# A Strassen matmul with its own scheduler: DMA rates and queue shares by stage, s2 in a11's place, one more second-level product

## The chip, the cores and the metric

The kernel runs on one core of a Trainium2 chip. The metric is the device time in microseconds of one execution. A matmul's rate is set by TensorE (PE); VectorE (DVE) and ScalarE (ACT) make the operands and take the results out of the accumulator banks (PSUM); GpSimd (POOL) issues the loads of the fp32 inputs, which are cast to fp16 on their way into the on-chip memory; SyncE (SP) issues all other DMAs. Both issue to the same 16 DMA engines.

## The reference

```python
def reference(a, b, bias):          # a 4096 x 4096, b 4096 x 4096, float32
    return np.tanh(np.matmul(a, b) + bias)
```

## The kernel before

**The sums.** The output is made in four panels of 1024 columns. A panel's product is made by Winograd's form of Strassen's scheme: a pair of row tiles (2 x 128 rows) and the two halves of the inner dimension give a11, a12, a21 and a22, the panel gives b11 to b22, and with s1 = a21 + a22, s2 = s1 - a11, s3 = a11 - a21, s4 = a12 - s2 and t1 to t4 likewise there are seven products: P1 = a11 b11, P2 = a12 b21, P3 = s4 b22, P4 = a22 t4, P5 = s1 t1, P6 = s2 t2, P7 = s3 t3. Two pairs form a *duo*, which is worked on together. A product of a duo is 2 x 16 matmuls of 512 columns (`product`, L817). It can be split once more by the same scheme over the duo's two pairs (a *fine* or second-level product): seven parts p1 to p7 of eight matmuls of 256 columns each (`fine`, L848, and `fine_product`, L832). For that VectorE makes half sums of the left side (ya, za of a11; ys, zs of s3 and s1; `fine_left`, L663) and quarter sums of the right side (f1, f2, f4 and one in place; `fine_right`, L802).

**The stages.** The opening computes the first 1024 rows of the first panel in plain matmuls (L2041). Then six duos finish the first panel; `STEEP` (L63) says how many products of each duo are fine: none for the first, then P1, then P1 and P7, then P1, P7 and P5. The second and third panels are made together in *wide* passes (`wide_pass`, L1710; class `Wide`, L1542), all products fine, with 512 columns to a part; seven products of eight duos, 56 in all. The last panel runs in two passes (`pass_one`, L1353, and `pass_two`, L1436) with 256 columns to a part; in the tables below its start is at about 1083 us.

**A duo of the first panel** (`run_duo`, L1036). POOL loads rows of a ("nat"), VectorE turns them (STREAM_TRANSPOSE, L498) into a11, a12, a21, a22. The order of TensorE is P1 (with, when it is fine, a product of the duo before as a filler between its parts p2 and p4), a second product that was held back from the duo before, P2, P7 and P6 by turns, P5, and then the tail P3, P4, P4, P3, of which the last two are held back for the next duo. A fine P7 runs p1, p5, p7, p6, p2, then P6 of the first pair as its filler, then p4 and p3, then P6 of the second pair. Three small sums of 256 columns (`ps<-ps,parts`, `parts<-ps,parts`) after the parts p6 and p2 make the banks ready for p4. After P5, `after_p5` (L1017) adds p7 to the bank and so frees it for P3.

**What is stored.** For the later panels, a11, a12, a22 and s2 of each pair (and some half sums) are stored to device memory by SP (`keep`, L590; in the traces `a<-a`, `s<-s`, `a<-ya`). Before, s2 has a buffer of its own in `natural` (L547), and s4 is later made in s2's place (`work`, L938). VectorE must wait for the store before it writes there.

**What sets the order.** Every operation is recorded first, with the buffers that it reads and writes and an estimated duration. A planner (`Plan.schedule`, L237) then plays the program through: TensorE's order is fixed as recorded; every other engine takes the ready operation with the nearest due time that finds room in 51 places on chip (`fits`, L277). A DMA is modelled by a rate, a fixed wait, and, when POOL and SP both have transfers under way, by a share for each (`rates`, L297). The order that comes out is the program's order on each engine, and each engine then runs in that order. So numbers of the model do not change what is computed; they change what stands behind what. `NEAR` (L32) says how far ahead of the matmul a load of b stops competing for places with what is due sooner.

```python
            soft_, hard = pipes["POOL"], pipes["SP"]
            part = SHARE[hard[0][1].kind]
            return [(soft_, part), (hard, 1 - part)]
```

Of the kernel before, what the change touches and what calls it, by code (L numbers as in the profile page):

```python
# [10 lines left out]
P = 128  # L11
# [4 lines left out]
T = 16  # L16
TB = 4
# [32 lines left out]
PLAIN = (0, 0, 0, 0)  # L50
SMALL = 7
LONG = 1.07
OVER = False
TWICE = True
RING = 8
DMA = {'POOL': (382140.0, 3.8), 'LATER': (386100.0, 4.8), 'in': (372240.0, 4.6), 'out': (376200.0, 4.3), 'open': (368280.0, 4.2)}
# [17 lines left out]
WIDE_EARLY = {'P1': (11.0, 70), 'P2': (11.0, 80), 'P6': (11.0, 100), 'P7': (8.0, 120), 'P4': (11.0, 70), 'P5': (11.0, 50), 'P3': (18.0, 100)}  # L74

# [68 lines left out]
class Op:  # L144
    __slots__ = (
        "parts", "n", "eng", "dur", "lag", "emit", "preds", "succs", "bufs", "nbytes", "hw", "soft", "early", "lead", "reach", "far",
        "unsent", "flying", "flow", "wait", "kind",
        "due", "left", "start", "done", "ready",
# [3 lines left out]
class Plan:  # L152
# [13 lines left out]

    def add(self, eng, dur, emit, reads=(), writes=(), nbytes=0, hw=True, soft=None, early=0.0, lead=0.0, reach=1e9, after=None, faster=1.0):
        early, far = early if isinstance(early, tuple) else (early, self.FAR)
        op = Op()
# [67 lines left out]
    def schedule(self):  # L237
# [163 lines left out]
def kernel(  # L401
# [113 lines left out]

    def load_rows(tl, srcs, nbytes, lead=0.0, faster=1.0):
# [7 lines left out]
        add("POOL", 4 * 0.55, emit, (), (tl,), nbytes=nbytes, hw=False, lead=lead, faster=faster)  # L524

    def natural_rows(pair, r, s, soft=None):
# [4 lines left out]
        for u in range(2):  # L531
# [5 lines left out]

            load_rows(tl, srcs, P * T * P * 4, NAT_LEAD if soft else 0.0, LONG)
            for h, name in enumerate(names if r == 0 else names[::-1]):
# [6 lines left out]

    def natural(pair, kept, own=False, spare=()):  # L547
        s = {}
# [188 lines left out]

    def load_b(buf, c, k0, nt, j=None, early=0.0, faster=1.0):

# [4 lines left out]
        def emit():  # L744
# [9 lines left out]
            "POOL", 4 * 0.55, emit, (), (buf,),  # L754
            nbytes=nt * P * n * 4, hw=False, early=early, faster=faster,
        )
# [953 lines left out]
    def wide_pass(c, held):  # L1710
# [5 lines left out]
        def load(name, at_=parts):  # L1716
            r, j = int(name[1]) - 1, int(name[2]) - 1
            for blk, i in at_:
                if not i:
                    bufs = [new(name, [P, 2, 2, NB], atoms=2 * TB) for _ in range(2)]  # L1720
                    for h in range(2):
                        raw[name, blk, h] = Block(bufs, h)
                load_b(raw[name, blk, 0].bufs[i], c + j, r * T + blk * TB + 2 * i, 2, early=soon[0], faster=LONG)

# [254 lines left out]
    def both_columns(h, blk):  # L1979
# [4 lines left out]
        for i, buf in enumerate(bufs):  # L1984
            load_b(buf, 0, h * T + blk * TB + 2 * i, 2)

# [167 lines left out]
    for c in range(NC):  # L2154
# [44 lines left out]
        for i, pairs in enumerate(duos):  # L2199
# [75 lines left out]
```

## Time and profile before

| | before |
|---|---|
| median of 3 runs | 1440.67 us (1439.12 to 1443.03) |
| the profiled execution | 1442.41 us; its span 1440.7 us |
| TensorE busy | 1423.2 us, 8384 matmuls |
| VectorE, ScalarE, GpSimd busy | 1070.7, 389.2, 325.4 us |
| granted TensorE clock | 0.999 |
| HBM read, written | 329.25 MB, 150.21 MB |

The span runs from the first to the last instruction of one profiled execution. "x" counts instructions. A row of the timeline has the start, the time that the group took, the engine, the line, what is written and read, the count, and in brackets how long the engine had been idle before it and what ended that. Names like `parts` or `b_209` are those of the first buffer that held a place: another buffer can be in it by then.

### The profile page before, as it was taken

The numbers are of one execution on the slowest core, as the hardware profiler recorded it, in microseconds if no ns is written. First come the engines' busy times: TensorE is split into PE (matmuls) and PEld (weight loads), VectorE is DVE, ScalarE is ACT, GpSimd is POOL, SyncE is SP. The second block draws the span as 40 slices with busy tenths as digits, with TensorE's granted clock in tenths as the row PEclk, the third lists the DMA queues.
The fourth block names the chain that finished last, engine by engine and source line by source line (L and its number), as shares of the span: only waits on it lengthen the run. The fifth ranks groups of instructions, "written<-read, shape, count | busy, mean of one in ns | idle before, by whom it ended". The sixth has DMA issues, their size and how long they took to land.

```text
span 1440.7 us, 22498 instructions
## 1 busy us (share of the span) xinstructions
PE 1423.2 (99%) x8384; PEld 819.5 (57%) x8384; DVE 1070.7 (74%) x1587; ACT 389.2 (27%) x740; POOL 325.4 (23%) x613
## 2 busy tenths in 40 slices
PE   9999999999999999999999999999999999999998
PEld 4444545555544444444444444444446888888887
DVE  3349976767885576796567778988687689997866
ACT  3111211221233223311111133233323332234443
POOL 8754343144353341100112130000120220000000
PEclk9999999999999999999999999999999999999999
DMA  9999999698999999897889899899999898789873
GB/s 175 183 228 284 245 268 287 163 237 208 266 264 309 260 284 313 291 368 268 266 286 310 280 293 380 332 390 330 329 325 342 237 276 284 256 277 321 308 285 134
DMA packets 168062, 401.30 MB, mean 279 GB/s; under 512 B 25488, under 2 KB 44432, under 8 KB 167952
## 3 DMA queue, kind: packets, MB, share of 16 engines
q1 hardware_dynamic: 104976, 320.12, 61.0%
q0 software_dynamic: 62976, 79.73, 33.3%
q8 instruction: 66, 1.08, 0.3%
q14 instruction: 44, 0.36, 0.1%
HBM read 329.25 MB, written 150.21 MB: 333 GB/s over the span
## 4 chain that ended last, share of the span: by engine, by line
PE 76%; DMA 11%; DVE 3%; issue 1%; SPq 0%; POOL 0%; ACT 0%; DVEq 0%; POOLq 0%; ACTq 0%
PE ps L1564 44%; PE ps L839 25%; PE ps L824 6%; DMA b<-in_b_dram 3%; DMA a<-parts 2%; DMA s<-s 2%; DMA out_dram<-parts 1%; DMA nat<-in_a_dram 1%; DMA a<-o 1%; DVE a L498 1%; DMA s<-parts 1%; DVE parts L465 1%; DVE s L465 0%; SPq L586 0%; DVE ps L465 0%
## 5 line engine op out<-in xcount | busy, mean ns | idle before, releaser
L751 POOL DMA_DIRECT2D b<-in_b_dram x320 | 169.8, 535 | 621.1 <-DMA out_dram<-u 163.3
L468 ACT COPY ps<-ps 128x512 f32<-128x512 f32 (+1 forms) x215 | 100.4, 467 | 448.2 <-PE ps L1564 310.9
L522 POOL DMA_DIRECT2D nat<-in_a_dram x224 | 118.5, 533 | 215.5 <-PE ps L839 57.5
L465 DVE TENSOR_TENSOR parts<-ps,parts 128x256 f32<-128x256 f32 (+1 forms) x128 | 72.0, 563 | 83.3 <-PE ps L1564 51.9
L465 DVE TENSOR_TENSOR u<-ps,u 128x512 f32<-128x512 f32 x160 | 105.8, 685 | 24.0 <-PE ps L1564 23.2
L2041 PE MATMUL ps<-b,o 128*128 128x512 f16 x512 | 111.3, 379 | 0.1
L468 ACT COPY parts<-ps 128x256 f32<-128x256 f32 (+1 forms) x148 | 68.3, 465 | 144.1 <-DVE ps L465 48.1
L1564 PE MATMUL ps<-b,zs 128*128 128x512 f16 x448 | 105.8, 379 | 0.0
L1564 PEld LDWEIGHTS <-ya 128*128 128x128 f16 x624 | 61.0, 98 | 73.6
L465 DVE TENSOR_TENSOR ps<-ps,parts 128x256 f32<-128x256 f32 (+1 forms) x149 | 81.7, 553 | 26.8 <-PE ps L1564 18.5
L824 PEld LDWEIGHTS <-s 128*128 128x128 f16 x576 | 56.2, 98 | 67.5 <-issue 2.0
L498 DVE STREAM_TRANSPOSE a<-nat 128x512 uint32<-128x512 uint32 x112 | 73.1, 689 | 21.1 <-DMA nat<-in_a_dram 16.1
L1564 PEld LDWEIGHTS <-xa 128*128 128x128 f16 x512 | 50.1, 98 | 60.2
L1564 PEld LDWEIGHTS <-zs 128*128 128x128 f16 x512 | 50.1, 98 | 60.2
L2041 PEld LDWEIGHTS <-o 128*128 128x128 f16 x512 | 49.8, 98 | 60.1 <-ACT o L2086 0.6
L824 PEld LDWEIGHTS <-a 128*128 128x128 f16 x480 | 46.9, 98 | 57.2 <-DVE a L498 2.1
L824 PE MATMUL ps<-t,s 128*128 128x512 f16 x352 | 78.1, 379 | 0.0
L1564 PE MATMUL ps<-b,za 128*128 128x512 f16 x320 | 75.6, 379 | 0.0
L486 ACT ACTIVATE parts<-ps 128x512 f32<-128x512 f32 x52 | 31.0, 597 | 160.6 <-PE ps L824 61.2
L465 DVE TENSOR_TENSOR b<-b,b 128x2048 f16<-128x2048 f16 (+2 forms) x76 | 68.0, 909 | 0.4 <-DMA b<-in_b_dram 0.3
L824 PE MATMUL ps<-b,a 128*128 128x512 f16 x288 | 63.8, 379 | 1.7 <-DVE a L498 1.6
L465 DVE TENSOR_TENSOR o<-ps,u 128x512 f32<-128x512 f32 x64 | 43.3, 688 | 29.0 <-PE ps L1564 27.2
(163 smaller groups left out, 2585.2 us busy)
## 6 DMA issues: line engine op xcount, KB each, us to landing
b<-in_b_dram POOLq DMA_DIRECT2D x320, 128.0 KB, 7.8
ya<-a SPq DMA_DIRECT2D x70, 512.0 KB, 6.5
xa<-a SPq DMA_DIRECT2D x70, 512.0 KB, 7.2
u<-U SPq DMA_DIRECT2D x64, 512.0 KB, 6.8
nat<-in_a_dram POOLq DMA_DIRECT2D x224, 128.0 KB, 7.9
U<-u SPq DMA_DIRECT2D x48, 512.0 KB, 7.2
ys<-s SPq DMA_DIRECT2D x46, 512.0 KB, 5.3
xs<-s SPq DMA_DIRECT2D x46, 512.0 KB, 5.5
```

What stands on the lines that cost most here:

```text
L465: dve(n, lambda: nc.vector.tensor_tensor(out=o(), in0=x(), in1=y(), op=op), reads, writes, wide, **kw)
L468: act(n, lambda: nc.scalar.copy(o(), x()), reads, writes, **kw)
L486: act(NB, lambda: nc.scalar.activation(o[ALL], src[ALL], TANH), (src,), (o,), soft=2.0)
L498: nc.vector.transpose(dst[ALL].rearrange("P t m -> P (t m)").bitcast(pair32).rearrange("P (U m) -> P U m", m=P)[:, ds(t0 // 2, nu), ds(row ...
L522: nc.gpsimd.dma_start(out=tl[(ds(q * QP, QP), *key)], in_=src)
L751: nc.gpsimd.dma_start(out=dst.rearrange("p t j n -> p t (j n)") if j is None else dst, in_=src)
L824: nc.tensor.matmul(bank[ALL], left_tile(left, k + t + shift), rb.tile(t), start=start and k == t0 and t == 0, stop=k + t == t0 + nt - 1, s ...
L839: nc.tensor.matmul(bank[ALL, HALF[half]], left_tile(buf, at_ * TP + i * TB + t), rb.tile(t), start=False, stop=i == 1 and t == TB - 1, ski ...
L1564: nc.tensor.matmul(bank[ALL, cols], left_tile(buf, at_ * TP + i * TB + t), rb.tile(t, half), start=start and not (i or t), stop=i == 1 and ...
L2041: nc.tensor.matmul(bank[ALL], left_tile(left, t), rb.tile(tb), start=start, stop=stop, skip_group_check=True,)
```

## The change

- The planner's DMA rates and waits stand in one table by stage (opening, rest of the first panel, the rest), with a kind of its own, "LONG", for POOL's loads with long runs (the rows of a, b two panels wide); the shares of the two queues stand in a table by stage, by long or short runs of the load, and by the kind of SP's transfer. 0.8 us are added to every wait.
- `STEEP`: the third duo of the first panel has two fine products instead of one (P7 with P1).
- `OVER`: in the second to fifth duo s2 is no longer made in `natural`, but after P1 in a11's place (`natural_late`); s3 is made earlier in exchange. s4 is made in s2's place as before, which is a11's now.
- `HOLD` keeps one more partial sum of the last panel on chip, `TURN` lets values of the wide passes stay on chip for up to 5 products instead of 3, `TOGETHER` no longer runs the last two duos of the kernel by turns. SP issues four transfers of 512 KB less: one store and one load of a state, two loads of a value u.
- `NEAR`, `FARTHER`, `AFTER`, `SMALL` and the lead of P1 and P2 in the wide passes are other numbers. With all this the order of DVE, ACT and SP is another from the opening to the end; POOL issues the same loads in the same order, but for the first load of a, which now stands ahead of the first loads of b.

```diff
-NEAR = 12.0
+NEAR = 10.0
...
-FARTHER = (50, 65, 40, 40)
+FARTHER = (50, 65, 40, 50)
...
-AFTER = (6, 6, 6, 6)
-HOLD = (1, 1, 1, 2)
+AFTER = (6, 6, 6, 7)
+HOLD = (1, 1, 1, 3)
...
-NAT_LEAD = 3.0
+NAT_LEAD = 2.0
...
-SMALL = 7
-LONG = 1.07
-OVER = False
+SMALL = 4
+OVER = True
...
-DMA2 = {'POOL': (382140.0, 4.0), 'LATER': (386100.0, 4.8), 'in': (372240.0, 4.6), 'out': (384120.0, 3.9)}
+SPEED, SLACK = 1.0, 0.8
+RATES = (
...
+    {"POOL": (375e3, 3.9), "LONG": (403e3, 3.9), "in": (396e3, 3.4), "out": (395e3, 3.5)},
+)
+SHARES = (
...
+    ((0.39, 0.45, 0.47), (0.44, 0.55, 0.58)),
...
-SHARE = (0.31, 0.51, 0.43)
...
-STEEP = ((0, 1, 1, 2, 2, 3), (), ())
+STEEP = ((0, 1, 2, 2, 2, 3), (), ())
...
-TOGETHER = (0, 0, 0, 2)
+TOGETHER = (0, 0, 0, 0)
...
-TURN = 3
+TURN = 5
...
         if nbytes:
-            kind = "LATER" if not hw and early else ("open", "POOL")[self.open > 0] if not hw else "out" if soft is not None else "in"
-            rate, op.wait = (DMA, DMA, DMA2)[self.open][kind]
-            op.flow = nbytes / rate / faster
+            kind = ("POOL", "LONG")[long] if not hw else "out" if soft is not None else "in"
+            rate, wait = RATES[self.open][kind]
+            op.flow, op.wait = nbytes / (rate * SPEED), wait + SLACK
+            op.share = SHARES[self.open][long]
...
-            part = SHARE[hard[0][1].kind]
+            part = soft_[0][1].share[hard[0][1].kind]
...
-        if OVER and not own:
+        if over:
             if kept:
                 keep(pair, s, BASIS[:2], spare=spare, soft=3.0)
             asum(s, "s3", "a11", "a21", SUB, over="a21")
...
-            d.a = [natural(p, p in early, i == 0, SPARE if p % 2 and duo not in WHOLE else ()) for p in d.pairs]
-            for name in BASIS if i == 0 else () if OVER else BASIS[1:]:
+            over = OVER and 0 < i < len(duos) - 1
+            d.a = [natural(p, p in early, i == 0, SPARE if p % 2 and duo not in WHOLE else (), over) for p in d.pairs]
+            for name in BASIS if i == 0 else () if over else BASIS[1:]:
                 sigma(name, duo, d.a)
```

The lines that `load_rows`, `natural_rows`, `load_b` and `both_columns` change only hand on `long=True` in place of a factor.

**How the order moves, first place.** VectorE in the second duo, around its P5 (205 us in the trace). `ps_276` and `ps_274` are banks of the two pairs in the order before, `ps_269` and `ps_267` in the order after; `parts<-ps_274` and `parts<-ps_267` are the first pair's sums of `after_p5`; `s_1760<-a_1624,s_1760` and `a_1383<-a_1622,a_1383` make the second pair's s4 in s2's place, `a_1401<-a_1606,a_1401` the first pair's. Before:

```order
L465 TENSOR_TENSOR ps_276<-ps_247,bias 128x512
L465 TENSOR_TENSOR ps_247<-ps_247,parts 128x512
L465 TENSOR_TENSOR s_1760<-a_1624,s_1760 128x2048
L465 TENSOR_TENSOR parts<-ps_274,parts 128x512
L498 STREAM_TRANSPOSE a_1809<-nat 128x2x8x32
```

After, the second pair's s4 stands behind the first pair's sum and ahead of the second pair's alone:

```order
L473 TENSOR_TENSOR ps_269<-ps_245,bias 128x512
L473 TENSOR_TENSOR ya_1820<-a_1772 128x1024
L473 TENSOR_TENSOR a_1401<-a_1606,a_1401 128x2048
L473 TENSOR_TENSOR parts<-ps_267,parts 128x512
L506 STREAM_TRANSPOSE a_1785<-nat 128x2x8x32
L473 TENSOR_TENSOR ya_1820<-ya_1820,a_1785 128x1024
L473 TENSOR_TENSOR za_1861<-a_1785,a_1772 128x1024
L473 TENSOR_TENSOR za_1861<-a_1785,ya_1820 128x1024
L473 TENSOR_TENSOR ps_245<-ps_245,parts 128x512
L473 TENSOR_TENSOR a_1383<-a_1622,a_1383 128x2048
L473 TENSOR_TENSOR parts<-ps_269,parts 128x512
```

The sum that frees the first pair's bank has moved ahead of the second pair's s4, and the half sums of the next duo's P1 stand between.

**Second place.** VectorE in the fourth duo, around the three small sums of its fine P1 (269 us in the trace). `a_23..<-nat` are transposes of that duo's rows, the rows that write or read `ps` with 128x256 are the small sums, `s_2388` and `s_2398` its s1. Before:

```order
L498 STREAM_TRANSPOSE a_2319<-nat 128x2x8x32
L465 TENSOR_TENSOR ps_257<-ps_279,parts 128x256
L498 STREAM_TRANSPOSE a_2345<-nat 128x2x8x32
L465 TENSOR_TENSOR ps_255<-ps_281,parts 128x256
L465 TENSOR_TENSOR ps_257<-ps_255,parts 128x256
L498 STREAM_TRANSPOSE a_2335<-nat 128x2x8x32
L465 TENSOR_TENSOR s_2388<-a_2319,a_2327 128x2048
L465 TENSOR_TENSOR s_2398<-a_2335,a_2345 128x2048
```

After, the same three sums, and the first of the twelve transposes that now stand behind them:

```order
L473 TENSOR_TENSOR za_2324<-a_2261,a_2245 128x1024
L473 TENSOR_TENSOR za_2324<-a_2261,ya_2289 128x1024
L473 TENSOR_TENSOR ps_259<-ps_279,parts 128x256
L473 TENSOR_TENSOR ps_257<-ps_281,parts 128x256
L473 TENSOR_TENSOR ps_259<-ps_257,parts 128x256
L506 STREAM_TRANSPOSE a_2419<-nat 128x2x8x32 x2
L506 STREAM_TRANSPOSE a_2430<-nat 128x2x8x32 x2
L506 STREAM_TRANSPOSE a_2444<-nat 128x2x8x32
L506 STREAM_TRANSPOSE a_2453<-nat 128x2x8x32
```

Transposes that stood ahead of the small sums and between them have moved behind.

**Third place.** VectorE at the start of the last panel (1095 to 1107 us in the trace). `f2b` and `f3b` are quarter sums of b21, which wait for its loads, `parts<-ya` and `za` half sums of a left side, and the rows with `ps` and 128x256 the small sums of P1's fine parts. Before:

```order
L465 TENSOR_TENSOR ps_255<-ps_257,edge 128x256
L676 TENSOR_TENSOR za_8981<-xa_8787,ya_8768 128x2048
L465 TENSOR_TENSOR f2b_8908<-b_8796,f1b_8826 128x1024
L465 TENSOR_TENSOR f3b_8915<-b_8796,b_8667 128x1024
L465 TENSOR_TENSOR parts<-ya_8814 128x1024
L676 TENSOR_TENSOR za_9023<-xa_8839,ya_8814 128x2048
L465 TENSOR_TENSOR parts<-ps_257,parts 128x256
L465 TENSOR_TENSOR ps_257<-ps_255,parts 128x256
```

After:

```order
L473 TENSOR_TENSOR ps_257<-ps_259,edge 128x256
L684 TENSOR_TENSOR za_9010<-xa_8854,ya_8839 128x2048
L473 TENSOR_TENSOR f2b_8932<-b_8806,f1b_8833 128x1024
L473 TENSOR_TENSOR f3b_8956<-b_8806,b_8678 128x1024
L473 TENSOR_TENSOR parts<-ps_259,parts 128x256
L473 TENSOR_TENSOR ps_259<-ps_257,parts 128x256
```

The half sum and the sum of 2048 that stood between f3b and the small sums have moved ahead of f2b.

More of the change, by code (lines that the diff above doesn't have):

```diff
@@ L146 @@
         "parts", "n", "eng", "dur", "lag", "emit", "preds", "succs", "bufs", "nbytes", "hw", "soft", "early", "lead", "reach", "far",
-        "unsent", "flying", "flow", "wait", "kind",
+        "unsent", "flying", "flow", "wait", "kind", "share",
         "due", "left", "start", "done", "ready",
@@ L165, in buf, with add @@
         return buf
-    def add(self, eng, dur, emit, reads=(), writes=(), nbytes=0, hw=True, soft=None, early=0.0, lead=0.0, reach=1e9, after=None, faster=1.0):
+    def add(self, eng, dur, emit, reads=(), writes=(), nbytes=0, hw=True, soft=None, early=0.0, lead=0.0, reach=1e9, after=None, long=False):
         early, far = early if isinstance(early, tuple) else (early, self.FAR)
@@ L514, in left_tile, with load_rows @@
         return pairs_of(buf, t - t % 2)[:, t % 2]
-    def load_rows(tl, srcs, nbytes, lead=0.0, faster=1.0):
+    def load_rows(tl, srcs, nbytes, lead=0.0, long=False):
         def emit():
@@ L522, in emit @@
                 nc.gpsimd.dma_start(out=tl[(ds(q * QP, QP), *key)], in_=src)
-        add("POOL", 4 * 0.55, emit, (), (tl,), nbytes=nbytes, hw=False, lead=lead, faster=faster)
+        add("POOL", 4 * 0.55, emit, (), (tl,), nbytes=nbytes, hw=False, lead=lead, long=long)
     def natural_rows(pair, r, s, soft=None):
@@ L545, in natural_rows, with natural @@
                 add("DVE", turn_time(1024), emit, (tl,), (s[name],), soft=soft)
-    def natural(pair, kept, own=False, spare=()):
+    def natural(pair, kept, own=False, spare=(), over=False):
         s = {}
@@ L754, in load_b @@
             "POOL", 4 * 0.55, emit, (), (buf,),
-            nbytes=nt * P * n * 4, hw=False, early=early, faster=faster,
+            nbytes=nt * P * n * 4, hw=False, early=early, long=long,
         )
@@ L1722, in load @@
                         raw[name, blk, h] = Block(bufs, h)
-                load_b(raw[name, blk, 0].bufs[i], c + j, r * T + blk * TB + 2 * i, 2, early=soon[0], faster=LONG)
+                load_b(raw[name, blk, 0].bufs[i], c + j, r * T + blk * TB + 2 * i, 2, early=soon[0], long=True)
         def total(name, x, y, op, over, at_=parts):
@@ L1984, in both_columns @@
         for i, buf in enumerate(bufs):
-            load_b(buf, 0, h * T + blk * TB + 2 * i, 2)
+            load_b(buf, 0, h * T + blk * TB + 2 * i, 2, long=True)
     for v in (0, 1, 2, 3, *(4 + i for i in H1)):
```

12 lines of the change are left out of this document (8 added, 4 removed).

## The prediction

> **What bounds the kernel now.** I read the page first, then the table by stretches, then the waits of TensorE, and last the timeline around each of those waits. The rows of the page:
>
> ```profile
> span 1440.7 us, 22498 instructions
> PE 1423.2 (99%) x8384; PEld 819.5 (57%) x8384; DVE 1070.7 (74%) x1587; ACT 389.2 (27%) x740; POOL 325.4 (23%) x613
> ...
> GB/s 175 183 228 284 245 268 287 163 237 208 266 264 309 260 284 313 291 368 268 266 286 310 280 293 380 332 390 330 329 325 342 237 276 284 256 277 321 308 285 134
> ```
>
> TensorE is busy for 99% of the span; 17.5 us of it are not matmul. So there are two ways to gain: fewer matmuls, or less of those 17.5 us. The table by stretches (span, then PE, PEld, DVE, ACT and POOL busy, clock, DMA share, GB/s) gives the pace:
>
> ```profile
> 100.00:150.00 50.00, 48.27 (x224) 21.62 (x223) 44.77 (x66) 7.10 (x12) 22.88 (x43) 1.00 1.09 286
> ...
> 600.00:700.00 100.00, 100.00 (x465) 45.30 (x463) 76.39 (x106) 16.79 (x28) 8.40 (x16) 1.00 0.89 305
> ...
> 900.00:1000.00 100.00, 100.00 (x465) 45.30 (x463) 89.37 (x125) 30.80 (x41) 0.00 (x0) 1.00 0.94 345
> ...
> 1300.00:1350.00 50.00, 50.00 (x461) 44.78 (x459) 40.15 (x62) 19.45 (x46) 0.00 (x0) 1.00 0.90 314
> ```
>
> A matmul of 512 columns takes 100/465 = 0.215 us, one of 256 columns 50/461 = 0.1085 us, and where PE is full nothing that other engines do can show in the time. What TensorE waited for (total, times, longest):
>
> ```profile
> PE ps L839 <- DVE ps L465: 5.1, 3, 1.9
> PE ps L839 <- DVE a L465: 1.9, 1, 1.9
> PE ps L824 <- DVE a L498: 1.6, 1, 1.6
> PE ps L824 <- DVE parts L465: 1.5, 1, 1.5
> PE warm L1960 <- DVE zeros L1954: 1.4, 1, 1.4
> PE ps L839 <- DVE zs L465: 0.7, 1, 0.7
> ```
>
> Without the start that is seven waits of 10.8 us in all, 1.5 us each, every one on VectorE. They are the whole prize beside the product.
>
> **The product.** A plain product of a duo is 32 matmuls of 512 columns, a second-level one 56 of 256: 32 x 0.215 = 6.88 us against 56 x 0.1085 = 6.08 us. The third duo's P7 turns from one to the other: **-0.8 us**. Its VectorE work (four half sums of the left side, three small sums) lies beside matmuls; the 16 sums of t3's quarters are only made one duo earlier.
>
> **Second wait, 205 us.** The queue's store of s2, the row of VectorE that it held, and TensorE:
>
> ```profile
> 192.44 0.87 SPq L586 DMA_DIRECT2D s<-s  x2
> ...
> 205.26 1.23 DVE L465 TENSOR_TENSOR s<-a,s 128x2048 f16<-128x2048 f16 x1 [5.15 <-DMA s<-s]
> 206.40 0.68 DVE L465 TENSOR_TENSOR parts<-ps,parts 128x512 f32<-128x512 f32 x1
> ...
> 207.14 3.61 PE L824 MATMUL ps<-b,s 128*128 128x512 f16 x16 [1.46 <-DVE parts L465]
> ```
>
> s4 of the second pair goes into s2's place, so it waits until s2 has been stored (12.8 us after the issue), and the sum behind it, which empties the bank that P3 wants, waits with it. In the order after, that s4 (`a_1383`) stands behind the first pair's sum (`parts<-ps_267`) and four rows later; only the second pair's sum, wanted two products on, is left behind it. **-1.5 us**; bounds -1.5 and 0.
>
> **Third wait, 269 us.** A transpose whose load was late stood between TensorE and two small sums:
>
> ```profile
> 270.08 0.71 DVE L498 STREAM_TRANSPOSE a<-nat 128x512 uint32<-128x512 uint32 x1 [2.78 <-DMA nat<-in_a_dram]
> 270.71 0.87 DVE L465 TENSOR_TENSOR ps<-ps,parts 128x256 f32<-128x256 f32 x2
> ...
> 271.63 1.03 PE L839 MATMUL ps<-f4b,a 128*128 128x256 f16 x8 [1.90 <-DVE ps L465]
> ```
>
> After, the three sums stand side by side with 12 transposes behind them: **-1.9 us**. What is late next is P7 of that duo, which needs zs. Behind the three sums stand 12 transposes, 4 sums of 2048 and 4 of 1024, by these rows 0.65, 1.16 and 0.61 us each:
>
> ```profile
> L498 DVE STREAM_TRANSPOSE a<-nat 128x512 uint32<-128x512 uint32 x112 | 73.1, 689 | 21.1 <-DMA nat<-in_a_dram 16.1
> ```
> ```profile
> 116.82 4.26 DVE L465 TENSOR_TENSOR t<-b,t 128x1024 f16<-128x1024 f16 x7
> ```
> ```profile
> 272.11 2.32 DVE L465 TENSOR_TENSOR s<-a,a 128x2048 f16<-128x2048 f16 x2
> ```
>
> 12 x 0.65 + 4 x 1.16 + 4 x 0.61 = 14.9 us. TensorE has until then 64 matmuls of 512 (13.8 us) and 32 of 256 (3.5 us), 17.2 us, less the 1.2 us in which the sums themselves are made: 16.0 us. The cover is 1.1 us; a load as late as the 2.78 us above would cost 1.7 us. I take nothing here and count it among the new waits below.
>
> **Fourth and fifth, 377 and 381 us** (the last duo's P7). Its s3 was late:
>
> ```profile
> 378.01 1.22 DVE L465 TENSOR_TENSOR a<-a,a 128x2048 f16<-128x2048 f16 x1
> ...
> 379.29 1.05 PE L839 MATMUL ps<-b,a 128*128 128x256 f16 x8 [1.87 <-DVE a L465]
> ```
>
> Of the rows between P1's small sums and this s3, two sums of 1024 (one of them the second half of a12's) are now placed behind it: 2 x 0.61 = 1.2 us. The rest of the 2.6 us stays unless loads land earlier: **-1.2 us**; bounds -2.6 and 0.
>
> **Sixth and seventh, 1097 and 1105 us** (the third panel's first products). Loads of b came late, and small sums waited behind the rows that use them:
>
> ```profile
> 1057.50 4.28 POOL L751 DMA_DIRECT2D b<-in_b_dram  x8 [8.04 <-DVE ps L465]
> ```
> ```profile
> 1094.70 0.69 DVE L465 TENSOR_TENSOR f2b<-b,f1b 128x1024 f16<-128x1024 f16 x1 [2.02 <-DMA b<-in_b_dram]
> ...
> 1102.67 0.69 DVE L465 TENSOR_TENSOR f2b<-b,f1b 128x1024 f16<-128x1024 f16 x1 [2.75 <-DMA b<-in_b_dram]
> ...
> 1106.62 1.03 PE L839 MATMUL ps<-f4b,xa 128*128 128x256 f16 x8 [1.83 <-DVE ps L465]
> ```
>
> POOL stood 8.04 us before these loads, until a sum of VectorE gave a place free. NEAR falls from 12 to 10, so fewer places are kept back for what is due soon, and a load may take one sooner; 2.0 of the 8.04 us are enough for the first wait. For the second the order alone does it: behind its f2b stand f3b and then the small sums, where a half sum and a sum of 2048 stood between (0.61 + 1.16 = 1.8 us less, on a wait of 1.83). The two waits are 5.1 - 1.9 = 3.2 us; I leave 0.3: **-2.9 us**. Bounds: -3.2, and -1.8 where the loads come no sooner.
>
> **First wait, 124 us.** It only changes its name:
>
> ```profile
> 126.56 3.63 PE L824 MATMUL ps<-b,a 128*128 128x512 f16 x16 [1.57 <-DVE a L498]
> ```
>
> The transpose moves ahead of the bias row and two b sums, but the sum that P2 needs (`ps<-ps,bias`) then has those two b sums ahead of it and one more half sum: the same work, on an engine that is busy 44.77 of 50 us there. **0**, bounds -1.6 and 0.
>
> **What the change adds.** In four duos s2 is now made after P1, in a11's place, so its store starts later, and s4 waits for that store. a11's own store goes out once a11 has been turned, ahead of P1, so that the place is free in time and costs nothing. In the third duo the second pair's s2 comes behind the small sums of the fine P7: 1.2 us for these after P7's fifth part, and 1.2 us for s2 itself. From the end of that part to P3 TensorE has 64 matmuls of 512 columns and 16 of 256, 15.5 us. The landing of such a store, by the DMA issues of 200 to 260 us and then of 250 to 300 us:
>
> ```profile
> s<-s SPq DMA_DIRECT2D x2, 256.0 KB, 11.1
> ```
> ```profile
> s<-s SPq DMA_DIRECT2D x2, 256.0 KB, 4.7
> ```
>
> With 11.1 us: 2.4, then 0.8 for the two issues (0.87 in the row of 192 us), 11.1, 1.2 for s4 and 0.6 for the sum behind it, 16.1 us against 15.5: a wait of 0.6 us. With the 12.8 us of the second wait it is 2.3 us, with 4.7 none. The third duo lies in the first stretch: **+0.6 us**. The four loads and stores that go (two of u, one pair of state) take 2 MB off 401 MB in stretches where PE waits for nothing: 0. The last two duos of the kernel no longer alternate: 0, as the same rows stand for both and PE is full from 1300 to 1350 us; without that cover it is one more of the new waits below. At the opening one load of a is issued ahead of b; the second stays where it is and TensorE waits for that one too: 0.
>
> **New waits.** Every engine but POOL has a new order, and the wide passes need not stay without a wait. Between none and five of the mean 1.5 us (0 and 7.5), I take one, as the two covers above are thin: **+1.5 us**.
>
> Sum: -0.8 - 1.5 - 1.9 - 1.2 - 2.9 + 0.6 + 1.5 = -6.2 us. The profiled execution took 1442.41 us, 1.7 us around its span of 1440.7, so 1436.2 by it; it stood 1.74 us over the median of the three runs, 1440.67, from which the sum gives **1434.5 us**. A measurement of this kernel can tell about 0.3%, 4.3 us, from no change.
>
> **Rivals.** *The waits only move* (0.17). For it: the first wait, where the work ahead is the same, and VectorE at 44.77 of 50 us. Against it: five of the waits had a late DMA in front of VectorE, and the plan's new share of POOL's long loads, 0.44 to 0.58 where it was 0.31 to 0.51, fits what the two queues show from 200 to 260 us:
>
> ```profile
> q0 software_dynamic: 3609, 5.92, 58.4%
> q1 hardware_dynamic: 4062, 8.69, 40.1%
> ```
>
> Time: 1440.67 - 0.8 = 1439.9.
>
> *s2's store holds three duos* (0.10): if it takes 12.8 us in the third, fourth and fifth, three waits of 2.3 us stand where I have 0.6: +6.3, 1440.8. For it is the 11.1 us; against it the 4.7 us later on.
>
> *Loads are planned too fast in the wide passes* (0.09), the slower side. The plan takes 396 GB/s and 4.2 us for a left load where it took 372 and 4.6. The row of 900 to 1000 us moves 345 GB/s at 0.94 share, 367 at full share: a load of 524,288 bytes takes 1.43 us, not 1.32. Four loads a product, 56 products: if half of the products wait these 0.42 us, 11.8 us, 1446.3. It decides once VectorE has left sums ready less than 0.42 us ahead. Against it: two slices of the page moved 380 and 390 GB/s, and PE is full at 0.94 share today. The Trainium skill (DMA: Bandwidth & Descriptors, section Specifications) puts the HBM limit of one core at about 358 GB/s; by that the loads would be 0.14 us late each and the estimate 15.7 us, 1450.2. The slice of 390 GB/s stands against it, so the rule moves no chance here.
>
> **How the numbers follow.** Forecast 0.64, of which 0.06 lies above 1436.4, the line of 0.3%. Faster 0.58; within 0.06 + 0.17 + 0.10 = 0.33; slower 0.09. The range: every wait gone and none new is 1440.67 - 0.8 - 10.8 = 1429.1, so 1430 below; 1441.5 above takes in the first two rivals, and leaves out the third and a little of each end.
>
> **What would show it.** Right: no wait of TensorE near 205, 269 and 1105 us; f2b without a DMA wait; 8408 matmuls; the P7 of the last duo still late by about 1.4 us. Wrong: `s4` held by the store with `parts<-ps,parts` behind it in the third duo; the sum behind 12 transposes late for P7 in the fourth; PE waits between 400 and 1080 us.

## The result, and the profile after

| | before | after |
|---|---|---|
| median (6 runs each) | 1441.16 us (1439.12 to 1443.99) | 1433.83 us (1432.04 to 1435.75) |
| ratio of after to before | | 0.9947, 95% interval 0.9934 to 0.9961 |
| the profiled execution | 1442.41 us, span 1440.7 us | 1433.78 us, span 1432.1 us |

The change makes the kernel 7.3 us faster by the medians, 8.6 us by the two profiled executions. The page of after:

```profile
span 1432.1 us, 22563 instructions
PE 1422.2 (99%) x8408; PEld 822.2 (57%) x8408; DVE 1078.1 (75%) x1594; ACT 392.8 (27%) x746; POOL 325.3 (23%) x613
```

All 8408 matmuls are there, and TensorE's idle time is what shrank. What it waited for (total, times, longest):

```profile
PE ps L832 <- DVE parts L473: 2.1, 1, 2.1
PE ps L847 <- DVE a L473: 1.7, 1, 1.7
PE warm L1968 <- DVE zeros L1962: 1.4, 1, 1.4
PE ps L847 <- ACT ps L476: 0.4, 1, 0.4
```

The rows of before added up to 13.0 us, these add up to 5.6, so 7.4 of the 8.6 us are waits. All seven of before are gone, the one at 124 us too, and so are the 0.6 us of the opening. Two new ones have come. The first stands in the third duo, on VectorE (the rows of DVE in the timeline, then TensorE's):

```profile
250.45 1.23 DVE L473 TENSOR_TENSOR a<-a,a 128x2048 f16<-128x2048 f16 x1 [4.55 <-DMA s<-a]
251.59 0.68 DVE L473 TENSOR_TENSOR parts<-ps,parts 128x512 f32<-128x512 f32 x1
...
252.33 3.61 PE L832 MATMUL ps<-b,a 128*128 128x512 f16 x16 [2.11 <-DVE parts L473]
```

This is `s4` in a11's place: it waits 4.55 us for the store of s2, the sum that frees P3's bank stands behind it, and TensorE waits 2.11 us for that sum. The second new wait is the fourth duo's P7, whose s3 (`a<-a,a`) is made of transposes that stood behind a late load:

```profile
272.53 1.30 DVE L506 STREAM_TRANSPOSE a<-nat 128x512 uint32<-128x512 uint32 x2 [2.73 <-DMA nat<-in_a_dram]
...
279.75 1.23 DVE L473 TENSOR_TENSOR a<-a,a 128x2048 f16<-128x2048 f16 x1
...
281.04 1.05 PE L847 MATMUL ps<-b,a 128*128 128x256 f16 x8 [1.71 <-DVE a L473]
```

From 300 us to the end there is one wait, of 0.4 us.

### The profile page after: what moved, and what is told of

It is laid out like the page before. It is cut to its first block, busy times and chain, and to the rows that moved or that the text cites. A ratio compares the mean times of both kernels' runs of the same rounds, so it can differ in the third digit from the quotient of the medians.

```text
span 1432.1 us, 22563 instructions
## 1 busy us (share of the span) xinstructions
PE 1422.2 (99%) x8408; PEld 822.2 (57%) x8408; DVE 1078.1 (75%) x1594; ACT 392.8 (27%) x746; POOL 325.3 (23%) x613
## 4 chain that ended last, share of the span: by engine, by line
PE 76%; DMA 2%; DVE 1%; POOL 0%; issue 0%; ACT 0%; SPq 0%; DVEq 0%
PE ps L1572 45%; PE ps L847 25%; PE ps L832 6%; DMA nat<-in_a_dram 1%; DMA xa<-a 1%; DMA s<-a 1%; DVE a L473 0%; POOL nat L530 0%; DVE s L473 0%; DVE a L506 0%; DVE u L473 0%; ACT parts L1370 0%; DVE ys L473 0%; DVE parts L473 0%; DVE za L684 0%
## 5 line engine op out<-in xcount | busy, mean ns | idle before, releaser
L476 ACT COPY ps<-ps 128x256 f32<-128x256 f32 (+1 forms) x216 | 100.8, 467 | 443.0 <-PE ps L1572 306.0
L473 DVE TENSOR_TENSOR parts<-ps,parts 128x512 f32<-128x512 f32 (+1 forms) x129 | 72.6, 563 | 67.2 <-PE ps L1572 40.0
L832 PEld LDWEIGHTS <-a 128*128 128x128 f16 x704 | 68.8, 98 | 81.9 <-issue 2.4
L1572 PE MATMUL ps<-b,zs 128*128 128x512 f16 x448 | 105.8, 379 | 0.0
L1572 PEld LDWEIGHTS <-ya 128*128 128x128 f16 x624 | 61.1, 98 | 73.6
L832 PE MATMUL ps<-b,a 128*128 128x512 f16 x384 | 84.7, 379 | 2.1 <-DVE parts L473 2.1
L1572 PEld LDWEIGHTS <-zs 128*128 128x128 f16 x512 | 50.1, 98 | 60.2
L1572 PEld LDWEIGHTS <-xa 128*128 128x128 f16 x512 | 50.1, 98 | 60.2
L1572 PE MATMUL ps<-b,za 128*128 128x512 f16 x320 | 75.6, 379 | 0.0
L832 PE MATMUL ps<-t,a 128*128 128x512 f16 x320 | 72.3, 379 | 0.0
L1572 PEld LDWEIGHTS <-za 128*128 128x128 f16 x384 | 37.6, 98 | 45.3
L847 PEld LDWEIGHTS <-ya 128*128 128x128 f16 x592 | 57.9, 98 | 7.1
```

The costliest lines, as they stand in the source:

```text
L473: dve(n, lambda: nc.vector.tensor_tensor(out=o(), in0=x(), in1=y(), op=op), reads, writes, wide, **kw)
L476: act(n, lambda: nc.scalar.copy(o(), x()), reads, writes, **kw)
L832: nc.tensor.matmul(bank[ALL], left_tile(left, k + t + shift), rb.tile(t), start=start and k == t0 and t == 0, stop=k + t == t0 + nt - 1, s ...
L847: nc.tensor.matmul(bank[ALL, HALF[half]], left_tile(buf, at_ * TP + i * TB + t), rb.tile(t), start=False, stop=i == 1 and t == TB - 1, ski ...
L1572: nc.tensor.matmul(bank[ALL, cols], left_tile(buf, at_ * TP + i * TB + t), rb.tile(t, half), start=start and not (i or t), stop=i == 1 and ...
```

## The experiments

The change was taken apart into four: **R**, the table of rates, fixed waits and shares; **P**, the third duo's fine P7; **O**, s2 in a11's place; **N**, all the other numbers (NEAR, FARTHER, AFTER, HOLD, NAT_LEAD, SMALL, TOGETHER, TURN, the leads of P1 and P2). "Waits" is the sum of TensorE's rows in the waits of the profiled execution, without the opening. That execution can lie away from the median: in e1, e4, e10 and e12 it is 2.7 to 3.7 us below it, in e8 1.9 us, elsewhere it is within 1.3 us. Each ratio stands against runs of the kernel before on the same chip. The kernels ran on different chips, so times in us of two kernels are compared only roughly.

| kernel | parts | median us | ratio (95% interval) | waits us |
|---|---|---|---|---|
| before | none | 1441.16 | 1 | 11.0 |
| after | R P O N | 1433.83 | 0.9947 (0.9934 to 0.9961) | 4.2 |
| e1 | P O N | 1442.96 | 1.0006 (0.9995 to 1.0017) | 8.9 |
| e2 | R | 1429.89 | 0.9917 (0.9904 to 0.9930) | 0.3 |
| e6 | R, shares alone | 1432.77 | 0.9931 (0.9919 to 0.9942) | 1.1 |
| e7 | R, rates and waits alone | 1442.67 | 1.0004 (0.9993 to 1.0015) | 8.8 |
| e8 | R with 0.9 us for 0.8 | 1432.75 | 0.9929 (0.9916 to 0.9943) | 0.5 |
| e9 | R, new shares in the first panel only | 1432.79 | 0.9938 (0.9925 to 0.9950) | 2.0 |
| e12 | one share of 0.58 | 1460.40 | 1.0138 (1.0115 to 1.0161) | 19.4 |
| e5 | R P | 1431.98 | 0.9927 (0.9915 to 0.9939) | 1.4 |
| e3 | R P N | 1436.21 | 0.9956 (0.9943 to 0.9968) | 4.1 |
| e4 | R P N, O without the third duo | 1437.40 | 0.9963 (0.9949 to 0.9976) | 4.2 |
| e10 | R P O | 1439.89 | 0.9989 (0.9979 to 0.9999) | 5.9 |
| e11 | R O N | 1431.34 | 0.9927 (0.9915 to 0.9939) | 1.3 |

### The table, and everything but the table

**e1**, the kernel after with the old model of DMAs (its rates, fixed waits and one set of shares):

```diff
-            rate, wait = RATES[self.open][kind]
-            op.flow, op.wait = nbytes / (rate * SPEED), wait + SLACK
+            rate, op.wait = (DMA, DMA, DMA2)[self.open][kind]
+            op.flow = nbytes / rate / (1.07 if long else 1.0)
...
-            part = soft_[0][1].share[hard[0][1].kind]
+            part = SHARE[hard[0][1].kind]
```

> The kernel after, with the planner's old DMA rates, waits and queue shares; everything else new. Theory A (each wait has a place and a cause; the new rates and shares are what keeps late DMAs from standing in front of VectorE): waits behind late loads come back in the first panel, two or three of 1.5 to 2 us, and TensorE's waits sum to some 8 us where they are 4.2 without the start; 1438 us. Rival B (any new set of numbers deals the waits out anew, and this draw was a lucky one): as likely better as worse, 1432 to 1440, with the waits at places that neither kernel showed. In both, 8408 matmuls.

**e2**, the kernel before with the table alone: the same lines the other way round, `STEEP`, `OVER` and all other numbers old.

> The kernel before, with the new DMA rates, waits and queue shares alone; 8384 matmuls. Theory A: the waits near 205, 269 and 377 us go, those near 1097 and 1105 stay unless the rates alone bring the loads of b forward: 1441.2 - 1.5 - 1.9 - 2.6 = 1435.2 us, and 1438 where one new wait of 2 us comes in. Rival B: 1438 to 1444, no better than before on the whole. Rival C (the table only works together with the places that s2 in a11's place frees): 1440 to 1442, with the same waits of VectorE on the stores of s2.

Measured: without the table the rest of the change gains nothing (1.0006); the table alone gains more than the whole change (0.9917 against 0.9947, intervals just apart), 1429.89 us. It is the fastest kernel of this study. Behind the start, which takes 1.4 us in every kernel, one wait is left:

```profile
PE ps L847 <- DVE ps L473: 0.3, 1, 0.3
```

In e1 the waits are back:

```profile
PE ps L849 <- DVE ps L475: 3.0, 4, 1.1
PE ps L849 <- DVE a L475: 2.1, 1, 2.1
...
PE ps L834 <- DVE parts L475: 1.2, 1, 1.2
```

All four of the first row stand in the last panel, two of them at its start, and behind the last row is again s4, held by the store of s2, at 204 us:

```profile
1095.70 1.03 PE L849 MATMUL ps<-f4b,xa 128*128 128x256 f16 x8 [0.93 <-DVE ps L475]
...
1103.08 1.03 PE L849 MATMUL ps<-f4b,xa 128*128 128x256 f16 x8 [1.11 <-DVE ps L475]
```
```profile
204.47 1.23 DVE L475 TENSOR_TENSOR a<-a,a 128x2048 f16<-128x2048 f16 x1 [2.28 <-DMA s<-a]
```

Theory A had the cause right and its size too small in both. A lucky draw (B) fell: e1 lies above its range and e2 far below, and more than half of e1's waits stand where before has them (at 204, 376, 1095 and 1103 us). C fell with e2, where s2 is in its own place. One wait says nothing for the table: that of 124 us is gone in every kernel here with a new order, in e1 and e7 (below) as well; e12 alone has another there, on ScalarE.

### Which part of the table

**e6** keeps the old rates and fixed waits and takes the new shares (the opening's loads of b get the shares for short runs there, in the whole table those for long ones); **e7** does the reverse.

```diff
-            part = SHARE[hard[0][1].kind]
+            part = soft_[0][1].share[hard[0][1].kind]
```

> The kernel before with the new shares of the two queues alone; rates and waits old; 8384 matmuls. Theory D (it is the shares: POOL's long loads were given 0.31 to 0.51 where both queues transfer, and now 0.40 to 0.58, so the planner knows when a load of a really lands): the waits at 205, 269, 377, 1097 and 1105 us go, 1431 us. Theory E (it is the rates and fixed waits): the waits stay in number, 1439 to 1442 us. Rival B (a lucky draw): 1436 to 1444, with waits at other places.

> The kernel before with the new rates and fixed waits alone; one set of shares as before; 8384 matmuls. Theory D: the waits stay in number, 1439 to 1442 us. Theory E: they go, 1431 us. Rival B: 1436 to 1444, with waits at other places.

Measured: the shares alone 0.9931, the rates and fixed waits alone 1.0004. The waits of e7:

```profile
PE ps L848 <- DVE ps L474: 3.9, 1, 3.9
...
PE ps L833 <- DVE parts L474: 1.3, 1, 1.3
```

Its longest is of the kind of 269 us in before, small sums behind transposes of a late load, at 220 us:

```profile
221.66 0.71 DVE L507 STREAM_TRANSPOSE a<-nat 128x512 uint32<-128x512 uint32 x1 [3.88 <-DMA nat<-in_a_dram]
222.30 0.40 DVE L474 TENSOR_TENSOR ps<-ps,parts 128x256 f32<-128x256 f32 x1
```

Theory D holds: it is the shares. Whether the rates and waits add anything on top of them is not shown: e2 lies 2.9 us below e6 (1429.89 to 1432.77), but the two ran on different chips, the intervals overlap, and a tenth of a microsecond on the fixed waits moves e2 by as much (e8 below).

**e9** is e2 with the old shares from the second panel on.

```diff
-    ((0.32, 0.40, 0.45), (0.47, 0.55, 0.54)),
+    ((0.31, 0.51, 0.43), (0.31, 0.51, 0.43)),
```

> The kernel before with the new rates and waits throughout, the new shares in the opening and the first panel, and the old ones (0.31, 0.51, 0.43) from the second panel on; 8384 matmuls. Theory D (each stage's shares clear the waits of that stage): no wait near 205, 269 and 377 us, and waits back near 1097 and 1105 us or in the wide passes, 1 to 4 us in all: 1431 to 1434 us against 1429.9 with the new shares everywhere. Rival (the shares of the first panel do it all, since what is stored and where it lies is settled there): 1429.9 us, no wait over 0.5 us.

Measured 1432.79 us, within D's range; its five runs, 1432.56 to 1433.36, all lie above the five of e2, 1429.68 to 1430.80, though the two intervals overlap. The waits that came are in the wide passes (TensorE's line there is L1572), and the first panel has none behind the opening:

```profile
PE ps L1572 <- DVE ys L473: 0.8, 1, 0.8
PE ps L1572 <- DVE parts L473: 0.8, 1, 0.8
```

So three quarters of the gain stay where the new shares hold in the opening and the first panel only (0.0062 of 0.0083).

**e12** is the kernel before with one share, taken from its trace between 200 and 260 us, for all stages.

```diff
-SHARE = (0.31, 0.51, 0.43)
+SHARE = (0.58, 0.58, 0.58)
```

> The kernel before with one number changed: POOL's share where both queues transfer is 0.58 for every kind of SP's transfer and every stage (from 200 to 260 us of the trace before, 46 loads of POOL that read 2 x 5.92 MB of float32 beside 8.69 MB of SP: 11.84/20.53 = 0.58); rates and fixed waits old; 8384 matmuls. Theory D1 (what was wrong in the plan is that SP was believed too fast beside POOL's loads, and any share near the measured one mends it): most of the waits in the first panel go, 1432 to 1435 us, as with the table of shares alone (1432.8). Theory D2 (it takes the table: the shares differ by stage and by the run length of the load, and 0.58 is wrong for b's short runs and the wide passes): the waits of the first panel go and others come in the wide passes or the last panel, 1437 to 1443 us.

Measured 1.0138, slower. D1 fell. D2 has the places right and the size too small: in the first 400 us the six waits of before behind the opening, 7.8 us, are three of 3.0 us, and the price is paid later, where POOL loads other things:

```profile
PE ps L1564 <- DVE xa L465: 7.5, 1, 7.5
PE ps L1564 <- DVE parts L465: 6.1, 2, 5.7
```

The wait of 7.5 us stands at the end of the wide passes, where VectorE takes a row that needs a load of b for the last panel too early:

```profile
1085.45 0.69 DVE L465 TENSOR_TENSOR f1b<-b 128x1024 f16<-128x1024 f16 x1 [4.08 <-DMA b<-in_b_dram]
...
1089.38 1.22 DVE L465 TENSOR_TENSOR xa<-xa,xs 128x2048 f16<-128x2048 f16 x1
...
1090.66 3.59 PE L1564 MATMUL ps<-b,xa 128*128 128x512 f16 x8 [7.46 <-DVE xa L465]
```

The wait of 5.7 us ends at 592 us; there VectorE stood 4.15 us in front of a half sum, until a store of results had landed. Why the plan put it there was not followed.

A reason why one number can't do is in the queues of before. From 700 to 1040 us, then from 1040 to 1100 us (packets, MB, share of the 16 engines):

```profile
q1 hardware_dynamic: 28421, 99.04, 78.4%
q0 software_dynamic: 6233, 9.41, 16.7%
```
```profile
q1 hardware_dynamic: 4619, 16.82, 73.9%
q0 software_dynamic: 3429, 3.13, 32.0%
```

q0 is POOL's, and its MB count what lands as fp16, half of what is read. Read per packet: 2 x 5.92 MB / 3609 = 3.3 KB in the stretch of 200 to 260 us, 2 x 9.41 / 6233 = 3.0 KB in the wide passes, 2 x 3.13 / 3429 = 1.8 KB at the start of the last panel, whose loads have runs half as long. SP's packets are 2.1, 3.5 and 3.6 KB. If an engine takes a packet from each queue by turns, POOL's share is 3.3/5.4 = 0.61, 3.0/6.5 = 0.46 and 1.8/5.4 = 0.33. The new table has 0.44 to 0.58, 0.47 to 0.55, and 0.32 to 0.45 for short runs. The old shares left SP 0.49 to 0.69 where the packets leave it 0.39 beside the loads of a, so stores were planned to land too early; that fits s4, which stood where it waited 5.15 us for one. The Trainium skill (DMA: Bandwidth & Descriptors, section Queues, rings and completion order) says that each DMA engine goes round its queues packet by packet.

Two things bear this out in part. The bytes of 200 to 260 us give POOL 0.58, near the 0.61; but the bytes of a stretch are also what the program asked for, and in the other two stretches they give 0.16 and 0.27, so this is weak support. And e12, planned with 0.58 where the packets give 0.33, has its 7.5 us at that place. That the shares are the cause is shown by e6; that turns by packets make them is argued, as the turns were not measured alone, and whether a packet of the profile is one turn is not shown.

### A tenth of a microsecond

**e8** is e2 with `SLACK` 0.9 for 0.8.

> The kernel before with the new rates and shares, and 0.9 us added to every wait of the model instead of 0.8. Theory A (the model is right on the whole, so a tenth of a us changes rows but not the waits): 1429.5 to 1431.5 us, no wait of TensorE over 0.7 us but the start's. Rival B (the 1429.9 us are one draw of many): two to five waits of 1 to 2 us at new places, 1433 to 1440 us.

Measured 0.9929; behind the start the profiled execution has no wait above 0.5 us, the median lies 2.9 us over that of e2 and the intervals overlap. The waits stay away, as A says, though the median is above A's 1431.5. The profiled execution is the fastest of the five (1430.89 of 1430.89 to 1435.17), so what makes the others longer is not seen.

### The fine product and s2's place

**e5** adds the fine P7 to e2.

```diff
-STEEP = ((0, 1, 1, 2, 2, 3), (), ())
+STEEP = ((0, 1, 2, 2, 2, 3), (), ())
```

> The kernel before, with the new DMA rates, waits and shares, and with the third duo's P7 fine; s2 in its own place, all other numbers old; 8408 matmuls. Theory A (the product is worth 0.8 us by itself, and it is the fine P7 that leaves VectorE too little room in the third and fourth duo): against the 1429.9 us of the new rates alone, a wait of 1.7 to 4 us before the fourth duo's P7: 1429.9 - 0.8 + 2.9 = 1432 us. Rival (the waits that the kernel after has come from s2 in a11's place and from the other numbers): no wait of TensorE over 0.5 us, 1429.1 us.

Measured 1431.98 us: the time that A gave, but by luck. The wait that A put before the fourth duo's P7 is not there; in its place are 0.6 us on `f2t`, a quarter sum that the product brings into the third duo, 0.6 at 1136 us and 0.2 at P3, less than half of A's 2.9.

**e11** takes the fine P7 out of the kernel after.

> The kernel after with the third duo's P7 plain again, so without the second-level product; 8384 matmuls. Theory F: with no small sums ahead of s2 the store starts some 2.4 us sooner and P7 takes 0.8 us longer, so the wait before the third duo's P3 goes; the fourth duo's P7 stays late by up to 1.7 us, since the numbers are new: 1433.8 + 0.8 - 2.1 = 1432.5 us. Rival (the wait before the fourth duo's P7 hangs on the places that the fine product holds): it goes too, 1430.8 us. Rival B: 1436 or more.

Measured 1431.34 us against 1433.83 for after: both new waits are gone, one of 1.1 us is at 324 us. The rival, by which the fourth duo's P7 hangs on what the fine product holds, is nearest. So with and without O and N the fine product goes with 2.5 and 2.1 us more, where its matmuls are 0.8 us shorter. In each of the two pairs the intervals overlap, so a loss is not shown; a gain is not seen in either. What it does to the next duo is seen on POOL: the last of the fourth duo's loads of a, in e11 and in after:

```profile
254.69 0.53 POOL L530 DMA_DIRECT2D nat<-in_a_dram  x1 [0.61 <-DMA nat<-in_a_dram]
```
```profile
266.76 2.28 POOL L530 DMA_DIRECT2D nat<-in_a_dram  x4 [1.03 <-DMA nat<-in_a_dram]
```

In the kernels with the new shares and a plain P7 there (e2, e6, e8, e9, e11) the last of these loads is issued between 254.7 and 258.4 us, in the five with a fine one (after, e3, e4, e5, e10) between 265.6 and 268.5 us, some ten microseconds later. In four of those five P7 of the fourth duo then waits, 1.6 to 4.1 us; in e5, the earliest, it does not, and in e1, with the old table and its last load at 267.3 us, it does not either. So the late loads go with the fine product; a wait need not follow.

**e3** has s2 in its own place in all duos (`OVER = False`), **e4** in the third duo alone:

```diff
-            over = OVER and 0 < i < len(duos) - 1
+            over = OVER and 0 < i < len(duos) - 1 and i != 2
```

> The kernel after, with s2 in a buffer of its own again in all duos; 8408 matmuls. Theory A: the wait of 2.1 us before P3 of the third duo (VectorE behind the store of s2, 4.55 us) goes, since that store starts some 10 us sooner: 1433.8 - 2.1 = 1431.7 us. Rival C (s2 in a11's place frees one place of 51 for each pair, and the loads of a start sooner by that): loads of a land later, transposes stand in front of sums as at 269 us before, two more waits of 1.5 to 2 us: 1437 us.

> The kernel after, with s2 in a buffer of its own in the third duo alone (late in a11's place in the second, fourth and fifth); 8408 matmuls. Theory A: the wait of 2.1 us before the third duo's P3 goes, the wait of 1.7 us before the fourth duo's P7 stays: 1431.7 us. Rival B: the changed recording gives a new order of everything behind it, and the time lands anywhere from 1431 to 1437. Rival C: one place less in the third duo brings a wait of 1.5 to 2 us elsewhere in it: 1433.8.

Measured 1436.21 and 1437.40 us. In both the wait before the third duo's P3 is gone, as A said, and in neither is the time gained. The waits of e3 and of e4:

```profile
PE ps L847 <- DVE a L473: 4.1, 1, 4.1
```
```profile
PE ps L847 <- DVE a L473: 3.6, 2, 2.0
```

In e3 the fourth duo's P7 is 4.1 us late instead of 1.7, and in e4 the last duo's P7 is late again besides. A's step was right and its sum wrong; for e3, C came nearest (1437, by later loads), with one longer wait where it had two. For e4 the profiled execution took 1433.73 us, and five of the seven took 1436.65 to 1439.19, so its waits do not account for the median.

**e10** is the kernel after with N undone.

> The kernel after with the small numbers old again (NEAR, FARTHER, AFTER, HOLD, NAT_LEAD, SMALL, TOGETHER, TURN, the leads of P1 and P2): new rates and shares, the fine P7 of the third duo, and s2 in a11's place; 8408 matmuls. Theory F (s2 in a11's place behind the small sums of the fine P7 makes the wait of 2.1 us before the third duo's P3, whatever the numbers; the wait of 1.7 us before the fourth duo's P7 comes from the numbers): the first stays at 1.5 to 2.5 us, the second goes, 1433.8 - 1.7 = 1432.1 us. Theory G (both come from s2 in a11's place): 1433.8 us. Theory H (both from the numbers): 1430 us.

Measured 1439.89 us. All three theories fell: the wait before P3 is gone, though VectorE stands there too, for a shorter time,

```profile
247.82 1.23 DVE L473 TENSOR_TENSOR a<-a,a 128x2048 f16<-128x2048 f16 x1 [2.33 <-DMA s<-a]
```

and P7 waits 5.9 us in all, in the fourth and in the last duo:

```profile
PE ps L847 <- DVE a L473: 5.9, 2, 4.1
```

So in the kernels with s2 in a11's place behind the fine P7 its store holds VectorE, 4.55 us in after, 2.33 in e10 and 1.82 in e1 (at 250.69 us). TensorE saw 2.11 of the 4.55 and nothing of the other two, which fits a cover of some 2.4 us (an estimate: 4.55 - 2.11).

With O the numbers N gain 6.1 us (after against e10), without it they cost 4.2 (e3 against e5), each with its intervals apart. So neither has a price of its own. Which of the numbers does it, was not tried, nor R with O or with N alone.

## Why the prediction was right, and where it was not

The time was forecast at 1434.5 us and came out at 1433.83. The terms (predicted against measured, in the profiled executions):

| term | predicted us | measured us |
|---|---|---|
| wait at 124 us | 0 | -1.6, gone |
| at 205 us | -1.5 | -1.5, gone |
| at 269 us | -1.9 | -1.9, gone |
| at 377 and 381 us | -1.2 | -2.6, gone |
| at 1097 and 1105 us | -2.9 | -3.2, gone |
| s2's store in the third duo | +0.6 | +2.1 |
| other new waits | +1.5 | +1.7 and +0.4 |
| opening, other small ones | 0 | -0.8 |
| sum of waits | -5.4 | -7.4 |
| product | -0.8 | not resolved |

The nearness is in part luck: the sum of waits was 2.0 us too small, the product of 0.8 us is not seen, and the median of before stood 0.5 us higher over six runs than over the three from which the forecast was taken.

- **Right with its place and mechanism.** The waits at 205 and 269 us, by the rows that the order moved.
- **Right in its size by two slips that cancel.** The cover of the fourth duo's P7 was put at 1.1 us: "a load as late as the 2.78 us above would cost 1.7 us". The load was 2.73 us late, and the wait is 1.71. That wait was named and priced, and then left at nothing and counted among the new ones. But P7 begins with s3 (its wait ended with `a<-a,a`), not with zs, so three of the four sums of 1024, 1.8 us, did not have to fit; and the small sums ended 2.8 us after the first of the 32 matmuls of 256 began, where 1.2 us were taken:

```profile
261.86 1.04 PE L847 MATMUL ps<-f2b,ya 128*128 128x256 f16 x8
...
263.33 1.37 DVE L473 TENSOR_TENSOR ps<-ps,parts 128x256 f32<-128x256 f32 x3 [6.56 <-ACT parts L476]
```

- **Right in its mechanism, too small: s2's store.** The sum was 16.1 us against a cover of 15.5, and the wait came out at 2.1 us instead of 0.6. The rows in after, of TensorE and VectorE, and of the store (count, durations in ns, first and last start; the last line has the landing in us):

```profile
233.56 1.03 PE L847 MATMUL ps<-b,a 128*128 128x256 f16 x8
234.49 3.63 PE L832 MATMUL ps<-t,a 128*128 128x512 f16 x16
```
```profile
234.34 0.69 DVE L473 TENSOR_TENSOR parts<-a 128x1024 f16<-128x1024 f16 x1
...
234.95 1.09 DVE L473 TENSOR_TENSOR f4t<-b,f2t 128x512 f16<-128x512 f16 x3
235.95 0.43 DVE L473 TENSOR_TENSOR ps<-ps,parts 128x256 f32<-128x256 f32 x1
236.28 0.42 DVE L473 TENSOR_TENSOR f4t<-b,f2t 128x512 f16<-128x512 f16 x1
236.62 0.43 DVE L473 TENSOR_TENSOR ps<-ps,parts 128x256 f32<-128x256 f32 x1
...
237.43 1.22 DVE L473 TENSOR_TENSOR a<-s,a 128x2048 f16<-128x2048 f16 x1
```
```profile
L594 SPq DMA_DIRECT2D s<-a x3: 326/327/1962, 234.5 to 239.0; - x3
...
DMA to landing us min/median/max: 4.3/10.3/11.3
```

  The fifth part ends at 234.5, s2 at 237.43 + 1.22 = 238.65, 4.2 us later where 2.4 were reckoned. VectorE is busy throughout: ahead of s2 stand, besides the small sums, a half sum (`parts<-a`) and four quarter sums of t3 (`f4t`), some 1.8 us that the working did not have. It had put t3's quarter sums at nothing, as work beside matmuls that is only made earlier. The store is issued by 239.0 and lands in 11.3 us at most, as reckoned (11.1), so by 250.3, and s4 begins at 250.45.
- **Too small.** The waits at 124 and 377 us lay within their bounds (-1.6 and -2.6 at the far ends), so the removals came out 3.3 us larger and the new waits 2.1 us larger than forecast; the two errors offset in part. The last duo's P7, which was to stay 1.4 us late, is not late at all; why the wait at 377 us went whole was not taken apart. The wait at 124 us goes with any new order (above).
- **Wrong in its reason: NEAR.** "NEAR falls from 12 to 10, so fewer places are kept back" was to free the loads of b for 1097 and 1105 us. With NEAR at 12 and the new table (e2) both waits are gone, and `f2b` does not wait for a load there, nor in after. With NEAR at 10 and the old model (e1) `f2b` waits 2.47 and 2.22 us for loads of b, and the two waits are there, 0.93 and 1.11 us, with two more behind them: 3.0 us in all, where before had 3.2. So it is the table that clears them. The shares stood in the prediction only as a reason against a rival ("fits what the two queues show"); alone they give as much as the whole change.
- **Not borne out: the product.** -0.8 us with its VectorE work that "lies beside matmuls" left out what goes with it: the quarter sums ahead of s2's store, and the next duo's loads, some ten microseconds later on POOL. By the medians it goes with 2.1 and 2.5 us more, with overlapping intervals in each pair. Its 0.8 us of matmul can't be seen in TensorE's busy time, which differs by more between kernels of the same matmuls (1423.2 in before, 1421.8 in e2).
- **The rivals.** "The waits only move" has two new waits of TensorE against seven gone, and both came with the fine product; "s2's store holds three duos" holds in one. "Loads are planned too fast in the wide passes" fell: none of the waits of after lies there, and the page of the profile has 389 GB/s in one slice. The Trainium skill (DMA: Bandwidth & Descriptors, section Specifications) gives about 358 GB/s as the limit of one core; the measured slice lies above it.

```profile
GB/s 188 178 236 286 251 293 196 222 240 221 274 276 316 235 274 302 280 358 290 265 291 294 270 294 389 341 367 344 334 335 354 271 248 265 250 297 286 304 301 134
```

## What to carry to other kernels

Where a planner sets the order, give it the share of the DMA engines that each queue gets, by stage and by the run length of the load: here the shares alone were worth 9 us and cost nothing, and one share for all stages cost 18. Price a saved matmul together with the VectorE work that it brings, and look at when the next block's operands are loaded beside it. When a change has several parts, run the part that removes waits alone: here the parts that looked like savings took back a third of its gain.

## What the runs showed of the hardware

- **A long wait is paid twice.** In e12 the wait of 5.7 us ends at 592.2 us and that of 7.5 us at 1090.7; the clock of TensorE (the column behind the five engines) is at 0.50 for the next 4 us, with half the matmuls:

```profile
580.00:586.00 6.00, 6.00 (x30) 2.74 (x28) 0.69 (x1) 1.75 (x3) 2.29 (x5) 1.00 0.68 186
592.20:596.20 4.00, 4.00 (x10) 1.48 (x11) 2.86 (x4) 1.60 (x2) 0.00 (x0) 0.50 0.51 143
597.00:601.00 4.00, 4.00 (x20) 1.76 (x18) 3.15 (x5) 1.06 (x2) 0.00 (x0) 1.00 0.80 254
1091.00:1095.00 4.00, 4.00 (x11) 1.46 (x10) 2.17 (x4) 0.00 (x0) 1.61 (x3) 0.50 1.05 316
```

  So it is after the wait of 4.1 us in e3. After the one of 3.9 us in e7 (at 224 us) and the one of 4.1 us in e10 (at 377 us) the clock is at 0.57 and 0.59 over 4 us, while the one of 2.1 us in after leaves it at 1.00:

```profile
281.00:285.00 4.00, 3.90 (x19) 2.79 (x20) 3.97 (x7) 0.36 (x1) 0.00 (x0) 0.50 0.00 2
```
```profile
252.30:255.30 3.00, 2.97 (x14) 1.37 (x14) 2.93 (x5) 1.26 (x2) 0.52 (x2) 1.00 0.54 201
```

  By these clocks a wait of 4 us costs 1.6 to 2 us more than it lasts (an estimate: 4 us times what the clock lacks). The Trainium skill (TensorE: Matmul & The Clock Gate, section What's actually happening) has the clock halve after an idle window of some 3.4 us; these waits agree, as far as they go.
- **How far the runs of a kernel lie apart.** The five runs of e2, with 0.3 us of waits in its profile, lie within 1.1 us (1429.68 to 1430.80), the five of e8, with 0.5 us, within 4.3 us (1430.89 to 1435.17), the seven of e4, with 4.2 us, within 5.8 us (1433.43 to 1439.19). So few waits in one profile do not make a kernel steady; what does was not tried.
